# Feed-forward stage: the forms of x in the activations' tiles, made at the beginning, and pair 3 by seven products

## The chip, the cores and the metric

The kernel runs on one core of a Trainium2 chip. The metric is the device time of one launch in microseconds. The engines are named as in the profile: PE is TensorE, PEld its weight loads, DVE is VectorE, ACT is ScalarE, POOL is GpSimd, and SP is the engine that issues most loads.

## The reference

The reference is a trunk of two layers on 512 tokens with 1024 features, all in fp32. In each layer come a mixer (attention in layer 0, an mLSTM in layer 1), a cross-attention to 256 memory tokens, and a gated feed-forward network with a short convolution. Only the last part is touched:

```python
def conv_ffn(xn, w_up, conv_w, conv_b, w_down):
    h = causal_depthwise_conv(xn @ w_up, conv_w) + conv_b   # w_up: 1024 x 5632, 3 taps
    g, u = jnp.split(h, 2, axis=-1)
    return (jax.nn.gelu(g) * u) @ w_down                    # w_down: 2816 x 1024
...
        x = x + conv_ffn(rms_norm(x, ffn_norm[layer]), ffn_w_up[layer], ffn_conv_w[layer],
                         ffn_conv_b[layer], ffn_w_down[layer])
```

## The kernel before

Features lie on the partitions and the 512 tokens on the free axis, so `x` is eight tiles of 128 x 512. Every product of fp32 matrices is made of three matmuls (`mm3`): both operands are split into a rounded high part and a rest, and high x high, high x rest and rest x high are summed. The high part is a cast on ACT, the rest a subtraction on DVE.

The up projection has 5632 columns, taken as 22 pairs: pair p has the 128 gate columns of block p and the 128 linear columns of block 22 + p. A pair is computed in one of two ways.

`plain(p, fill)` makes two blocks of output, 128 features x 512 tokens each, over eight blocks of the input: 2 x 8 x 3 matmuls of 512 columns. Each weight block is loaded, cast and split (1024 columns), and each sum is evacuated on DVE with the norm's factor.

`seven(p, fill)` treats the pair as a product of two matrices of 2 x 2 blocks (two halves of the input features and two of the output, two halves of the tokens) and computes it with seven products of blocks in place of eight, in Winograd's form. A product is 4 x 3 matmuls of 256 columns. Its weights are A11 and A12 (`raw`, `f3`), S1 and S3 (`sa`, `f1`: a load, and a second load that POOL adds onto it in memory), S2 and S4 (`s2`, `s4`, formed on DVE in `sb`) and A22 (`a22`, loaded into `ra`). The results go through PSUM and the small sums `v`, `u2`, `u3`, `c11`, `c12`, `c21`, `c22` into `hs`, which one DVE instruction then scales with the norm's factor. The products `p1` to `p7` use half of the tokens of `xh`/`xl` (p1, p2, p3) or of the forms T1 to T4 of x (p4 to p7).

`forms(k, at)` makes these forms for the input blocks k and k + 4, once per layer: two scalings on ACT, sums and differences on DVE, a cast into `th[k]` and a subtraction into `tl[k]`. Before the change the scaled blocks lie in a tile of `hs` (two of them, which the pairs use in turn), and the sums in a tile of `sa` (three, which hold the loads of S1 and S3 for the seven pairs). `p6` of each seven pair waits for all forms, and so do the additions of the down projection to x.

`tail(p, ...)` follows each pair: the three taps (one on ACT, four instructions `c` at L1314 on DVE), gelu, the product, and the split into the activations' tiles `ah` and `al`, of which there are ten each. `down(c, m)` multiplies a chunk of four (the last one: six) of these by a block of the down projection and adds to x. Down projections of chunk 0 to 3 are put between the products of pairs from 5 on (`fill`), two to a pair as long as the queue has any; `due` says at which pair a chunk joins the queue. The last five wait till the pairs are done, and chunk 4 comes at the end.

The order of the work is planned twice. `Sched` is a list scheduler in Python: every step is a task on one engine with a duration, a due time, its dependences and the buffers that it takes (`act`=10, `hs`=2, `sa`=3, `h`=3 and others) in the order in which the tasks were added; it issues what can start first, by due time among equals. The framework then puts the instructions on the engines in that order of priority, where an instruction whose inputs are ready may pass an earlier one that waits, and tiles of a new stage may be filled as soon as the tiles of the old stage in the same memory are read for the last time. The tiles of the feed-forward stage are laid out in the order `th`, `tl`, `s2`, `a22`, `s4`, `ah`/`al`, `hs`, and then the others.

Before the change pairs 0 to 3 are plain and pairs 4 to 21 go by seven products. The forms are asked for behind pairs 0 and 1:

```python
        for p in range(22):
            ...
            (seven if p in SEVEN else plain)(p, fill if p >= 5 else lambda: None)
            if p < 2:
                for k in (2 * p, 2 * p + 1):
                    forms(k, clock[0] + 4.0 * (k % 2))
```

Of the kernel before, what the change touches and what calls it, by code (L numbers as in the profile page):

```python
# [9 lines left out]
F32 = mybir.dt.float32  # L10
F32R = mybir.dt.float32r
I32 = mybir.dt.int32
AF = mybir.ActivationFunctionType
ALU = mybir.AluOpType
# [8 lines left out]
NPAIR = DFF // P  # L23
CHUNKS = [(0, 4), (4, 4), (8, 4), (12, 4), (16, 6)]

SEVEN = (4, 5, 6, 7, 8, 9, 10, 11, 12, 13, 14, 15, 16, 17, 18, 19, 20, 21)
EPS = 1e-6

X_AT, X_STEP = 2.6, 0.6
# [32 lines left out]
class Plan:  # L62
# [11 lines left out]
    def add(self, fn, dur=0.0, deps=(), prio=None, take=(), free=(), chain=(), pre=(), after=0.0, order=(), load=(), st=None):  # L74
        it = Item(fn, dur, [d for d in deps if d is not None], len(self.items) if prio is None else prio, take, free, chain, pre, after, order, load, st)
        it.n = len(self.items)
        self.items.append(it)
        return it
# [151 lines left out]
class Builder:  # L230
# [924 lines left out]
    def ffn_steps(self, layer, mp):  # L1155
# [3 lines left out]
        nc, t = self.nc, self.t  # L1159
        sc = Sched(raw=3, h=3, s2=1, s4=1, a22=1, sa=3, sb=2, ra=1, hs=2, c=1, dr=2, v=1, u2=1, u3=1, act=10, acc=4, s=2, w=2)  # L1160
        add = sc.add
        tt = lambda n: 0.055 + 1.06e-3 * n
        act = lambda n: 0.1 + 0.83e-3 * n
        ACV, STT = 0.71, 0.66
        clock = [0.0]
        state = {}
        acts, acted = {}, {}
        HALF = [slice(0, 256), slice(256, 512)]
        pair = lambda a: a.rearrange("p (a b) -> p a b", a=2)
# [10 lines left out]
        def raw_tile(st, tag):  # L1180
            pool, n, bufs = RAWS[tag]
            st[tag] = self.til(pool, tag, (P, n), bufs=bufs)
            return st[tag]
# [76 lines left out]
        th, tl = ([mp.tile([P, 1024], F32R, name=f"t{i}{layer}{k}", tag=f"t{i}{k}") for k in range(4)] for i in "hl")  # L1260
        small_ = lambda tag: [self.til(mp, tag + i, dtype=F32R, bufs=1) for i in "hl"]
        act_ = lambda: tuple(self.til(mp, i, dtype=F32R, bufs=10) for i in ("ah", "al"))
# [5 lines left out]
        formed = []  # L1268
        hs2 = [mp.tile([P, 2, 514], F32, name=f"hs{layer}{i}") for i in range(2)]
# [2 lines left out]

        def forms(k, at):

            st = {}

            def scaled(j):
                if j == 0:
                    st["t"] = hs2[st["_hs"]][:, :, 2:514]
                nc.scalar.activation(st["t"][:, j, :512], self.x[k + 4 * j][:], AF.Identity, scale=self.col("ffn", layer * 8 + k + 4 * j))  # L1280

            def first():
                st["r"] = raw_tile(st, "sa")[:]
                tt_(out=pair(st["r"][:, :512]), in0=pair(st["t"][:, 0, :512]), in1=st["t"][:, :, 256:512], op=ALU.subtract)

            T1, T3, T2, T4 = (slice(256 * i, 256 * i + 256) for i in range(4))
            tt_ = nc.vector.tensor_tensor
            a = add("ACT", ACV, lambda: scaled(0), (), at, [("hs", st)])
            a = add("ACT", ACV, lambda: scaled(1), [a], at)
            a = add("DVE", tt(512), first, [a], at, [("sa", st)])  # L1290
            a = add("DVE", tt(256), lambda: tt_(out=st["r"][:, T2], in0=st["t"][:, 1, 256:512], in1=st["r"][:, T1], op=ALU.add), [a], at)
            a = add("DVE", tt(256), lambda: tt_(out=st["r"][:, T4], in0=st["t"][:, 1, 0:256], in1=st["r"][:, T2], op=ALU.subtract), [a], at, (), [("hs", st)])
            h = add("ACT", act(1024), lambda: nc.scalar.copy(th[k][:], st["r"]), [a], at)
            formed.append(add("DVE", tt(1024), lambda: self.sub(tl[k][:], st["r"], th[k][:]), [h], at, (), [("sa", st)]))


        def tail(p, st, deps, at):
# [187 lines left out]

        normed = None
        due = {4 * c + 5 + c // 3: c for c in range(4)}
        for p in range(22):
            if p in due:
                queue += [(due[p], m) for m in range(8)]  # L1490
            if p == 19:
                queue, late = queue[:-5], queue[-5:]
            (seven if p in SEVEN else plain)(p, fill if p >= 5 else lambda: None)
            if p < 2:
                for k in (2 * p, 2 * p + 1):
                    forms(k, clock[0] + 4.0 * (k % 2))
        queue += late
        while queue:
            fill()
        if layer == 0:  # L1500
            for m in range(8):
                e = down(4, m, 2)
                a = add("ACT", 1.2, lambda m=m: self.xprep(m, "mix", 1, state), [e], clock[0] + 3.0)
# [371 lines left out]
```

## Time and profile before

| | |
|---|---|
| time, median of 3 runs | 1487.87 us (1487.7 to 1488.3) |
| profiled execution: own time | 1488.21 us |
| profiled execution: span from first to last instruction | 1486.4 us |
| mean granted TensorE clock | 0.999 |
| busy PE / DVE / ACT / POOL | 1474.2 / 1207.3 / 814.7 / 61.6 us |
| first matmul of the feed-forward stage, layer 0 / layer 1 | 416.05 / 1134.68 us |

The profile is one execution. Times of the trace count from its first instruction. The page has a line for each engine with its busy time in 40 equal slices of the span, each digit a tenth; a timeline row has the start in us, the duration in us, the engine, the line of the kernel, the operation, output and inputs, and in brackets the idle time of the engine before it and what ended that. Many rows have the line of a helper: L284 to L286 are the three matmuls of `mm3`, L275 is the subtraction of every split.

### The profile page before, as it was taken

How to read it: one execution, taken by the hardware profiler on the slowest of the kernel's cores; microseconds unless marked ns; L12 is line 12 of the kernel's file. 1: busy time of each engine (PE TensorE's matmuls, PEld its weight loads, DVE VectorE, ACT ScalarE, POOL GpSimd, SP SyncE). 2: the span in 40 equal slices, each digit the busy share in tenths (PEclk: the TensorE clock that was granted, in tenths of full speed). 3: DMA queues.
4: the chain of work that ended last, by engine and by line, in shares of the span. 5: the costliest groups of instructions: out<-in, count | busy, mean ns of one | idle time of the engine just before them, and what ended most of it. 6: DMA issues, size and time to landing. Idle time of an engine off the chain costs nothing.

```text
span 1486.4 us, 22787 instructions
## 1 busy us (share of the span) xinstructions
PE 1474.2 (99%) x8570; PEld 1276.6 (86%) x8570; DVE 1207.3 (81%) x2332; ACT 814.7 (55%) x1372; POOL 61.6 (4%) x104
## 2 busy tenths in 40 slices
PE   9999999999999999999999999999999999999998
PEld 7888777888888999999888778888888899999987
DVE  7779795666679999999768857666567999999984
ACT  7777573444456555555446634444444655555554
POOL 0000130000001000000000000000000000000000
PEclk9999999999999999999999999999999999999999
DMA  5212223323237565662322222323323666656422
GB/s 196 86 63 79 86 79 121 122 78 128 72 131 201 163 150 168 157 157 77 92 96 86 71 99 77 108 85 119 123 71 121 169 171 157 171 154 160 117 67 78
DMA packets 62463, 174.94 MB, mean 118 GB/s; under 512 B 6800, under 2 KB 6800, under 8 KB 62352
## 3 DMA queue, kind: packets, MB, share of 16 engines
q1 hardware_dynamic: 56160, 153.48, 31.4%
q0 software_dynamic: 5184, 18.88, 7.5%
q8 instruction: 67, 1.10, 0.3%
q10 hardware_dynamic: 1008, 1.12, 0.2%
q14 instruction: 44, 0.36, 0.1%
HBM read 171.35 MB, written 2.10 MB: 117 GB/s over the span
## 4 chain that ended last, share of the span: by engine, by line
PE 81%; DVE 13%; ACT 2%; issue 2%; DMA 1%; ACTq 0%; DVEq 0%; SPq 0%
PE acc L284 16%; PE acc L285 16%; PE acc L286 16%; PE w L286 4%; PE w L284 4%; PE w L285 4%; DVE wl L275 3%; PE acc L345 3%; PE acc L347 2%; PE acc L346 2%; PE s L284 2%; PE s L285 2%; PE s L286 2%; DVE c L1314 2%; PE w L1660 1%
## 5 line engine op out<-in xcount | busy, mean ns | idle before, releaser
L284 PE MATMUL acc<-xh,wh 128*128 128x512 f32 (+1 forms) x800 | 284.2, 355 | 0.0
L286 PE MATMUL acc<-xh,wl 128*128 128x512 f32 (+1 forms) x800 | 279.6, 349 | 0.0
L285 PE MATMUL acc<-xl,wh 128*128 128x512 f32 (+1 forms) x800 | 279.4, 349 | 0.0
L275 DVE TENSOR_TENSOR wl<-raw,wh 128x1024 fp32r<-128x1024 f32 (+4 forms) x199 | 235.5, 1184 | 41.0 <-ACT wh L278 39.2
L278 ACT CAST wh<-raw 128x1024 fp32r<-128x1024 f32 (+1 forms) x135 | 139.4, 1035 | 162.7 <-PE acc L285 98.0
L286 PEld LDWEIGHTS acc<-xh,wl 128*128 128x128 f32 x800 | 150.2, 188 | 20.1
L285 PEld LDWEIGHTS acc<-xl,wh 128*128 128x128 f32 x800 | 150.4, 188 | 19.9
L284 PEld LDWEIGHTS acc<-xh,wh 128*128 128x128 f32 x800 | 150.3, 188 | 19.8
L1314 DVE SCALAR_TENSOR_TENSOR c<-hs,vec,c 128x512 f32<-128x512 f32 x176 | 129.5, 744 | 0.3
L286 PE MATMUL w<-ah,wl 128*128 128x512 f32 x304 | 119.0, 391 | 0.0
L284 PE MATMUL w<-ah,wh 128*128 128x512 f32 x304 | 118.7, 390 | 0.0
L285 PE MATMUL w<-al,wh 128*128 128x512 f32 x304 | 118.6, 390 | 0.0
L1307 ACT ACTIVATE c<-hs,vec 128x512 f32<-128x512 f32 x88 | 70.2, 813 | 46.9 <-DVE hs L1457 41.8
L1202 ACT CAST wh<-dr 128x512 fp32r<-128x512 f32 x64 | 39.5, 618 | 51.8 <-PE acc L285 16.7
L286 PEld LDWEIGHTS w<-ah,wl 128*128 128x128 f32 x304 | 57.1, 188 | 12.0
L284 PEld LDWEIGHTS w<-ah,wh 128*128 128x128 f32 x304 | 57.1, 188 | 10.5 <-ACT ah L1328 0.6
L285 PEld LDWEIGHTS w<-al,wh 128*128 128x128 f32 x304 | 57.1, 188 | 10.0
L284 PE MATMUL acc<-mem,wh 128*128 128x256 f32 (+1 forms) x192 | 61.5, 320 | 0.0
L286 PE MATMUL acc<-mem,wl 128*128 128x256 f32 (+1 forms) x192 | 61.0, 318 | 0.0
L285 PE MATMUL acc<-mem,wh 128*128 128x256 f32 (+1 forms) x192 | 60.8, 317 | 0.0
L526 DVE TENSOR_TENSOR x<-acc,x 128x512 f32<-128x512 f32 x32 | 22.1, 691 | 46.9 <-PE acc L286 46.9
L526 DVE TENSOR_TENSOR x<-w,x 128x512 f32<-128x512 f32 x72 | 49.2, 684 | 12.2 <-PE w L286 11.6
(390 smaller groups left out, 3950.7 us busy)
## 6 DMA issues: line engine op xcount, KB each, us to landing
raw<-in_up_dram SPq DMA_DIRECT2D x52, 512.0 KB, 3.4
sa<-in_up_dram SPq DMA_DIRECT2D x36, 512.0 KB, 4.3
sa<-in_up_dram POOLq DMA_DIRECT2D x36, 512.0 KB, 5.6
dr<-in_down_dram SPq DMA_DIRECT2D x64, 256.0 KB, 3.3
ra<-in_up_dram SPq DMA_DIRECT2D x36, 256.0 KB, 3.1
raw<-in_xk_dram SPq DMA_DIRECT2D x16, 512.0 KB, 3.3
raw<-in_wo_dram SPq DMA_DIRECT2D x16, 512.0 KB, 3.3
raw<-in_xq_dram SPq DMA_DIRECT2D x16, 512.0 KB, 3.3
```

The costliest lines, as they stand in the source:

```text
L275: self.nc.vector.tensor_tensor(out=lo, in0=v, in1=hi.bitcast(F32), op=ALU.subtract)
L278: self.nc.scalar.copy(hi, v)
L284: mm(out, wh, xh, start=first, stop=False, skip_group_check=parts)
L285: mm(out, wh, xl, start=False, stop=False, skip_group_check=parts)
L286: mm(out, wl, xh, start=False, stop=last, skip_group_check=parts)
L345: mm(ps, xh[k][:, ts], wh[:, ws], start=(k == 0), stop=False)
L346: mm(ps, xh[k][:, ts], wl[:, ws], start=False, stop=False)
L347: mm(ps, xl[k][:, ts], wh[:, ws], start=False, stop=(k == 7))
L526: self.nc.vector.tensor_tensor(out=self.x[m][:], in0=ps[:], in1=self.x[m][:], op=ALU.add)
L1202: nc.scalar.copy(st["wh"][:, :cols], st[tag][:, :cols])
L1307: nc.scalar.activation(st["c_"][:, j, :], hs()[:, j, 2:514], AF.Identity, scale=self.col("cw", (layer * 3 + 2) * 44 + blk), bias=self.col( ...
L1314: nc.vector.scalar_tensor_tensor(out=c, in0=hs()[:, j, n : n + 512], scalar=w, in1=c, op0=ALU.mult, op1=ALU.add)
```

## The change

Pair 3 is added to the pairs that go by seven products: 19 of 22. The forms are asked for ahead of all pairs, with due times 2, 4, 6 and 8. They take two of the ten tile pairs `ah`/`al` each in place of a tile of `hs` and one of `sa`: the first for the two scaled blocks, given back after the sums, the second for the sums. The four sums are four instructions of 256 columns (before: one of 512 and two of 256). The cast into `th` and the subtraction into `tl` are done in two halves of 512 (before: one of 1024 each).

```diff
-SEVEN = (4, 5, 6, 7, 8, 9, 10, 11, 12, 13, 14, 15, 16, 17, 18, 19, 20, 21)
+SEVEN = tuple(range(3, 22))
...
         def forms(k, at):
 
-            st = {}
+            st, su = {}, {}
+            two = lambda: [a[:].bitcast(F32) for a in act_()]
+            L, R = HALF
+            tt_ = nc.vector.tensor_tensor
 
             def scaled(j):
                 if j == 0:
-                    st["t"] = hs2[st["_hs"]][:, :, 2:514]
-                nc.scalar.activation(st["t"][:, j, :512], self.x[k + 4 * j][:], AF.Identity, scale=self.col("ffn", layer * 8 + k + 4 * j))
+                    st["t"] = two()
+                nc.scalar.activation(st["t"][j], self.x[k + 4 * j][:], AF.Identity, scale=self.col("ffn", layer * 8 + k + 4 * j))
 
             def first():
-                st["r"] = raw_tile(st, "sa")[:]
-                tt_(out=pair(st["r"][:, :512]), in0=pair(st["t"][:, 0, :512]), in1=st["t"][:, :, 256:512], op=ALU.subtract)
-
-            T1, T3, T2, T4 = (slice(256 * i, 256 * i + 256) for i in range(4))
-            tt_ = nc.vector.tensor_tensor
-            a = add("ACT", ACV, lambda: scaled(0), (), at, [("hs", st)])
+                su["r"] = two()
+                t, r = st["t"], su["r"][0]
+                tt_(out=r[:, L], in0=t[0][:, L], in1=t[0][:, R], op=ALU.subtract)
+                tt_(out=r[:, R], in0=t[0][:, R], in1=t[1][:, R], op=ALU.subtract)
+
+            def second():
+                t, (r, q) = st["t"], su["r"]
+                tt_(out=q[:, L], in0=t[1][:, R], in1=r[:, L], op=ALU.add)
+                tt_(out=q[:, R], in0=t[1][:, L], in1=q[:, L], op=ALU.subtract)
+
+            a = add("ACT", ACV, lambda: scaled(0), (), at, [("act", st)])
             a = add("ACT", ACV, lambda: scaled(1), [a], at)
-            a = add("DVE", tt(512), first, [a], at, [("sa", st)])
-            a = add("DVE", tt(256), lambda: tt_(out=st["r"][:, T2], in0=st["t"][:, 1, 256:512], in1=st["r"][:, T1], op=ALU.add), [a], at)
-            a = add("DVE", tt(256), lambda: tt_(out=st["r"][:, T4], in0=st["t"][:, 1, 0:256], in1=st["r"][:, T2], op=ALU.subtract), [a], at, (), [("hs", st)])
-            h = add("ACT", act(1024), lambda: nc.scalar.copy(th[k][:], st["r"]), [a], at)
-            formed.append(add("DVE", tt(1024), lambda: self.sub(tl[k][:], st["r"], th[k][:]), [h], at, (), [("sa", st)]))
+            a = add("DVE", 0.68, first, [a], at, [("act", su)])
+            b = add("DVE", 0.68, second, [a], at, (), [("act", st)])
+            for i, c in enumerate((a, b)):
+                w = slice(512 * i, 512 * i + 512)
+                c = add("ACT", act(512), lambda i=i, w=w: nc.scalar.copy(th[k][:, w], su["r"][i]), [c], at)
+                last = add("DVE", tt(512), lambda i=i, w=w: self.sub(tl[k][:, w], su["r"][i], th[k][:, w]), [c], at, (), [("act", su)] if i else ())
+            formed.append(last)
...
         due = {4 * c + 5 + c // 3: c for c in range(4)}
+        for k in range(4):
+            forms(k, 2.0+2.0*k)
         for p in range(22):
...
-            if p < 2:
-                for k in (2 * p, 2 * p + 1):
-                    forms(k, clock[0] + 4.0 * (k % 2))
```

## Prediction

> **What bounds the kernel now.** I read the page first, then the waits of TensorE (PE), then busy time by stretches of the first feed-forward stage, then single instructions.
>
> ```profile
> PE 1474.2 (99%) x8570; PEld 1276.6 (86%) x8570; DVE 1207.3 (81%) x2332; ACT 814.7 (55%) x1372; POOL 61.6 (4%) x104
> DVE  7779795666679999999768857666567999999984
> PE acc L284 <- DVE u L1433: 0.7, 4, 0.2
> ```
>
> PE is busy for 99% of the span, and the only thing in the two feed-forward stages that it is ever said to wait for is `u` on VectorE (DVE), four times. But the tenths of DVE stand at 9 through both feed-forward stages (slices 12 to 18 and 32 to 37), so two engines are full there at once. The stretches of layer 0 show where exactly; the columns are stretch, length, then busy time of PE, PEld, DVE, ACT and POOL, clock, DMA share and GB/s.
>
> ```profile
> 416.00:427.00 11.00, 11.00 (x53) 8.90 (x52) 9.79 (x26) 5.93 (x8) 0.00 (x0) 1.00 0.43 139
> 427.00:438.00 11.00, 11.00 (x50) 9.03 (x49) 9.37 (x15) 8.53 (x12) 0.00 (x0) 1.00 0.24 88
> 438.00:449.00 11.00, 11.00 (x50) 9.11 (x49) 10.05 (x16) 7.58 (x10) 0.69 (x1) 1.00 0.42 143
> 449.00:461.00 12.00, 12.00 (x54) 9.95 (x53) 12.00 (x18) 7.05 (x9) 1.17 (x2) 1.00 0.86 220
> 480.00:500.00 20.00, 20.00 (x147) 18.61 (x147) 19.99 (x35) 11.47 (x18) 0.86 (x1) 1.00 0.54 139
> 560.00:580.00 20.00, 20.00 (x143) 18.57 (x142) 20.00 (x35) 10.90 (x18) 1.71 (x2) 1.00 0.61 175
> 580.00:600.00 20.00, 20.00 (x151) 18.89 (x151) 19.61 (x36) 11.31 (x19) 0.85 (x1) 1.00 0.62 158
> 680.00:705.00 25.00, 24.92 (x206) 24.12 (x205) 24.99 (x43) 14.81 (x24) 0.00 (x0) 1.00 0.19 64
> 1145.60:1156.50 10.90, 10.90 (x49) 8.93 (x48) 9.29 (x15) 8.39 (x12) 0.00 (x0) 1.00 0.25 89
> ```
>
> PE is never idle here. DVE has 1.21 + 1.63 + 0.95 = 3.8 us to spare between 416 and 449, while the plain pairs run, then none up to 580, a little (0.39) in the stretch after, and none in 680 to 705. The layer 1 row shows the same picture (1.61 us spare). So a saving on PE counts in full only if DVE, which this change loads more, does not fall behind.
>
> **What the change removes on PE.** A plain pair is 48 wide matmuls, a pair by seven products 84 narrow ones (7 products, 4 blocks, 3 matmuls each).
>
> ```profile
> 442.21 0.39 PE L284 MATMUL acc<-xh,wh 128*128 128x512 f32 x1
> 447.65 0.39 PE L284 MATMUL acc<-xh,wh 128*128 128x512 f32 x1
> 1191.28 0.28 PE L284 MATMUL s<-xh,s4h 128*128 128x256 f32 x1
> 1192.64 0.28 PE L284 MATMUL s<-th,wh 128*128 128x256 f32 x1
> ```
>
> The first two rows are 24 wide matmuls apart: 5.44 us, 227 ns each, so a plain pair takes 10.88 us. The last two are one product of 12 narrow matmuls apart: 1.36 us, 113 ns each, so seven take 9.52 us. Pair 3 saves 1.36 us in each layer, 2.72 in all. This is the whole gain that PE can give, 0.18% of the time. The Trainium skill (TensorE: Matmul & The Clock Gate, section "Back-to-back issue gap") says that in a stream of weight loads and matmuls the spacing is about 131 ns at 512 columns and 81 ns at 128, so that narrow ones cost more for each column; by a straight line between (98 ns at 256, my estimate) pair 3 would become 84 x 98 - 48 x 131 = 1.9 us longer. This trace disagrees, with 227 and 113 ns.
>
> **What it adds on PE.** The pair that runs without down projections between its products (`fill` starts at pair 5) waits for its own sums:
>
> ```profile
> 469.56 1.21 DVE L275 TENSOR_TENSOR wl<-sa,wh 128x1024 fp32r<-128x1024 f32 x1
> 470.70 0.41 DVE L1433 TENSOR_TENSOR u<-acc,v 128x256 f32<-128x256 f32 x1
> 471.03 0.68 DVE L1324 TENSOR_TENSOR c<-c 128x512 f32<-128x512 f32 x1
> 470.71 0.28 PE L286 MATMUL acc<-th,s2l 128*128 128x256 f32 x1
> 471.16 0.39 PE L284 MATMUL acc<-th,a22h 128*128 128x256 f32 x1 [0.18 <-DVE u L1433]
> ```
>
> Between the last two rows 0.45 us pass where 0.11 would do: 0.34 us lost in pair 4, because `u3` stood behind a weight split on DVE. Now pairs 3 and 4 both run without down projections. I count the stall a second time: 0.34 in each layer, 0.68 in all, with bounds of nothing (the order may fall better) and twice that. A gain below nothing is excluded by no row, as the old stall may go too: that is a rival below.
>
> **What it adds on DVE.** The spacings of instructions that stand back to back, as each record overlaps the next a little:
>
> ```profile
> 474.17 0.68 DVE L275 TENSOR_TENSOR a22l<-ra,a22h 128x512 fp32r<-128x512 f32 x1
> 474.77 0.41 DVE L1433 TENSOR_TENSOR hs<-s,u 128x256 f32<-128x256 f32 x1
> 475.10 0.67 DVE L275 TENSOR_TENSOR s4l<-sb,s4h 128x512 fp32r<-128x512 f32 x1
> 475.70 1.21 DVE L1457 TENSOR_TENSOR hs<-hs,rb 128x1024 f32<-128x1024 f32 x1
> 476.84 0.41 DVE L1433 TENSOR_TENSOR u<-acc,v 128x256 f32<-128x256 f32 x1
> ```
>
> So 0.33 us for 256 columns, 0.60 for 512, 1.14 for 1024 (the split at 469.56 too). A plain pair has two splits of 1024 and two evacuations of 512: 3.48 us. A seven pair has two sums and three splits of 512, two splits of 1024, five sums of 256 and one scaling of 1024: 5 x 0.60 + 2 x 1.14 + 5 x 0.33 + 1.14 = 8.07. The taps are the same. That is +4.6 a layer. A form was 0.60 + 2 x 0.33 + 1.14 = 2.40 and becomes 4 x 0.33 + 2 x 0.60 = 2.52: +0.5 for four. DVE gets 5.1 us more in each layer, against 1.36 saved on PE.
>
> ```profile
> 462.90 0.36 ACT L1428 ACTIVATE v<-acc 128x256 f32<-128x256 f32 x1
> 463.16 0.61 ACT L1384 CAST s4h<-sb 128x512 fp32r<-128x512 f32 x1
> ```
>
> ScalarE gets three casts of 512, `v` and a copy of 256 more, 3 x 0.61 + 2 x 0.36 = 2.6 us; at 7.05 busy of 12.00 before pair 4 that is covered. SP gets the loads of pair 3 in other shapes, and POOL one more accumulating DMA.
>
> **What covers the DVE work: the move of the forms.** Where they run now, and why:
>
> ```profile
> L1271 POOL MEMSET hs<- x4: 102/103/103, 382.0 to 1132.0; 128x4 f32 x4
> L1280 ACT ACTIVATE hs<-x,vec x16: 706/716/722, 417.0 to 1166.3; 128x512 f32<-128x512 f32 x16
> 413.38 0.10 POOL L1271 MEMSET hs<- 128x4 f32 x1 [31.24 <-PE acc L285]
> 410.81 0.69 DVE L526 TENSOR_TENSOR x<-acc,x 128x512 f32<-128x512 f32 x1 [2.09 <-PE acc L286]
> 416.25 0.69 DVE L526 TENSOR_TENSOR x<-acc,x 128x512 f32<-128x512 f32 x1 [2.09 <-PE acc L286]
> 442.10 1.22 DVE L275 TENSOR_TENSOR tl<-sa,th 128x1024 fp32r<-128x1024 f32 x1
> 443.38 5.45 SPq L1188 DMA_DIRECT2D sa<-in_up_dram  x2
> ```
>
> Each tile waits for memory of the stage before. The first `hs` tile is free at 382.0, the second at 413.38, so the first form starts at 417.0 and the others queue behind `hs` slots that the pairs hold. The activations' tiles are laid out ahead of `hs`, over memory of the same attention tiles, so I take them to be free by about 382. Then a form can start when its two `x` are final. `x` 6 is written at 410.81, `x` 7 at 416.25, the ones before every 5.44 us; and DVE stands idle for 2.09 us in each such step. Four sums of 256 (1.32 us) fit into that. Forms 0 to 2 would put 4.0 us of DVE work before 416, where it costs nothing. The splits into `th` and `tl` cannot go there, since these tiles lie over what the last output projection still reads. What is left, 5.1 - 4.0 = 1.1 us a layer plus the 1.36 that PE gains, has the 3.8 us idle of 416 to 449 for cover. I price the DVE load at nothing. If neither cover were there it would be 5.1 a layer. The `sa` slots are also freed: today pair 4's load at 443.38 waits for a form's last read of `sa` (442.10 + 1.22), so pair 3's loads can go early.
>
> **The sum**: -2.72 + 0.68 = -2.04. The profiled execution's own time is 1488.21 us, so 1486.17; it stands 0.34 above the median of the runs, 1487.87, so 1485.8 as a median.
>
> **The rivals.** *DVE becomes the bound (slower).* Tiles come free too late or the order puts the forms' sums where DVE is full, and pairs 3 and 4, each 8.07 us and taps on top, run behind each other with no down projection to stretch them. For it: no idle DVE from 449 to 580. Against: the idle stretches above. It decides when more than 3.8 of the 5.1 us find no gap; then PE waits for `u`, `s2` and `hs`. With no move ahead of 416 and half of the idle time used, 5.1 - 1.9 = 3.2 a layer arrive late, 6.4 in all, which replaces the gain, as DVE then sets the end: 1494.3. Up to 1498.1 with no cover.
>
> *The entry of the stage is delayed (slower).*
>
> ```profile
> 417.60 0.71 ACT L506 ACTIVATE xh<-x,vec 128x512 fp32r<-128x512 f32 x1
> 418.34 0.75 DVE L507 SCALAR_TENSOR_TENSOR xl<-x,vec,xh 128x512 fp32r<-128x512 f32 x1
> 416.05 0.39 PE L284 MATMUL acc<-xh,wh 128*128 128x512 f32 x1
> ```
>
> Pair 0 needs `xl` 7 after seven blocks of 0.68 us, at 420.8; it is there at 419.1. If the six casts into `th` of forms 0 to 2 go ahead of `xh` 7 (form 3 needs `x` 7 itself), 6 x 0.61 = 3.7 us against 1.7 of slack, PE waits 2.0 a layer: 1485.8 + 4.0 = 1489.8. Against: `xh` 7 comes earlier in the program.
>
> *The gain is eaten.* Pair 3 waits for its own splits or the last `tl`, and DVE is that much later in 680 to 705, where it has nothing to spare: 0 to 1.4 a layer lost, time about 1487.2.
>
> *More gain than PE's share.* Freed `sa` slots and earlier forms also take away the 0.34 of pair 4 and the other waits for `u` (0.7 in all on the page): -2.72 - 1.4 - some ordering luck, 1483.7.
>
> *Narrow products bound by the weight load.* Were each spaced by the load's busy time (1276.6 us over 8570 loads, 149 ns on average), pair 3 would take 12.5 us, +1.6 a layer: 1491.1. The skill's rule above leans that way; the spacing of 113 ns in the 18 pairs that run so already leaves it 1%.
>
> **How the numbers follow.** Forecast 60%; eaten gain 15%; DVE bound 13%; entry delayed 5%; more gain 6%; weight load 1%. A difference under 0.2% (3 us) is about what a measurement of this kernel cannot tell from none, and PE's share is below it, so forecast and eaten gain are both "same": 0.75, faster 0.07, slower 0.18. The range leaves out the DVE bound and the larger gain (19%); its low end is PE's whole share with no second stall, 1485.1, less 0.5 for the spread of runs, its high end the weight load's price: 1484.6 to 1491.1.
>
> **What would show it.** Right: the matmuls with `th` number 19/18 of now; first sums of forms from about 400; DVE idle before 416 shrunk; PE waits for `u` still about 0.2 each. Wrong: PE gaps of over 1 us between 445 and 480 that end on DVE (`s2l`, `tl`, `u`), or a last `tl` after 451.

## The result: slower by 3.4 us, just above the range

The kernel after takes 1491.53 us (median of 10 runs, 1490.81 to 1493.35), the kernel before 1488.12 in the same runs: a ratio of 1.0024, 95% interval 1.0016 to 1.0032. The forecast was 1485.8, the range ended at 1491.1. TensorE (PE) does what was forecast, and VectorE (DVE) takes it back and more. The page of after, busy time and DVE's tenths:

```profile
PE 1474.5 (99%) x8642; PEld 1279.5 (86%) x8642; DVE 1215.5 (82%) x2366; ACT 821.4 (55%) x1390; POOL 64.5 (4%) x106
DVE  7779795666689999999778857666567999999984
```

PE runs 72 matmuls more, 84 narrow ones for 48 wide ones in each layer, in the same busy time (1474.2 before). A matmul's record (0.39 us) is longer than the spacing to the next start (0.227), so a start that is late by less than that still shows as busy. DVE has 8.2 us more (1207.3 before). The page hardly shows the damage. The stretches of layer 0 do (stretch, length, busy time of PE, PEld, DVE, ACT, POOL, clock, DMA share, GB/s), first two of the kernel before, then those of the kernel after:

```profile
405.00:416.00 11.00, 11.00 (x50) 9.13 (x49) 6.36 (x8) 4.40 (x6) 0.10 (x1) 1.00 0.31 109
461.00:480.00 19.00, 18.82 (x151) 18.06 (x150) 18.90 (x34) 11.89 (x20) 2.55 (x3) 1.00 0.85 215
```

```profile
405.00:416.00 11.00, 11.00 (x50) 9.11 (x49) 6.36 (x8) 4.42 (x7) 0.10 (x1) 1.00 0.34 110
416.00:427.00 11.00, 11.00 (x53) 9.03 (x52) 10.15 (x32) 10.77 (x18) 2.72 (x3) 1.00 0.97 282
427.00:438.00 11.00, 11.00 (x50) 9.06 (x49) 11.00 (x21) 8.29 (x12) 0.00 (x0) 1.00 0.74 182
438.00:449.00 11.00, 11.00 (x50) 9.12 (x49) 11.00 (x18) 6.02 (x8) 0.00 (x0) 1.00 0.28 95
449.00:461.00 12.00, 11.75 (x95) 11.18 (x93) 11.86 (x18) 7.81 (x12) 0.86 (x1) 1.00 0.46 115
461.00:480.00 19.00, 18.28 (x142) 17.40 (x143) 18.86 (x34) 9.12 (x17) 1.71 (x2) 1.00 0.69 183
```

Three things are to be seen. DVE's 3.8 us of idle time between 416 and 449 have shrunk to 0.85. The stretch ahead of 416 has not filled: 6.36 us of 11, with 8 instructions, as before. And behind 449 PE is now idle for 0.25 and 0.72 us in the last two stretches; before it was for nothing and for 0.18. What it waits for stands in PE's waits (us in total, times, longest), of which the first line is new:

```profile
PE s L286 <- DVE wl L275: 2.0, 4, 0.6
PE acc L284 <- DVE u L1443: 0.4, 2, 0.2
```

The four waits are one in pair 4 and one in pair 5 of each layer, before the first matmul of `p5` that reads `wl`, the low part of the split of `sa`. The first of them on PE, ScalarE and DVE:

```profile
460.47 0.28 PE L285 MATMUL acc<-xl,wh 128*128 128x256 f32 x1
461.15 0.38 PE L286 MATMUL s<-th,wl 128*128 128x256 f32 x1 [0.40 <-DVE wl L275]
455.78 1.05 ACT L1394 CAST wh<-sa 128x1024 fp32r<-128x1024 f32 x1 [0.67 <-PE acc L285]
457.41 0.74 DVE L1324 SCALAR_TENSOR_TENSOR c<-hs,vec,c 128x512 f32<-128x512 f32 x1
458.07 0.69 DVE L275 TENSOR_TENSOR s2l<-sb,s2h 128x512 fp32r<-128x512 f32 x1
458.67 0.68 DVE L1334 TENSOR_TENSOR c<-c 128x512 f32<-128x512 f32 x1
459.27 0.69 DVE L1406 TENSOR_TENSOR sb<-sb,raw 128x512 f32<-128x512 f32 x1
459.88 1.22 DVE L275 TENSOR_TENSOR wl<-sa,wh 128x1024 fp32r<-128x1024 f32 x1
```

The cast that `wl` needs is done at 456.83; `wl` starts 3.05 us later, behind a sum `u`, a tap, a split, the product with the gate and a sum into `sb`. DVE has no idle time between these rows: it is a backlog.

To sum this up I take the feed-forward stages from the start of the first matmul to that of the last:

| | layer 0 | layer 1 |
|---|---|---|
| before | 416.05 to 755.97: 339.92 us | 1134.68 to 1475.90: 341.23 us |
| after | 416.01 to 756.76: 340.75 us | 1135.72 to 1478.44: 342.71 us |

The matmuls of the change take 1.36 us less in each layer at 227 ns (512 columns) and 113 ns (256 columns) from start to start. So what lies between starts beyond these spacings, PE's lost time, grew by 2.2 us in layer 0 and 2.8 in layer 1. That is 5.0 more, against 2.72 saved: 2.3. The first matmuls of the last group and the final stores, before and then after:

```profile
1478.14 1.95 PE L1723 MATMUL acc<-ident,x 128*128 128x128 f32 x16
1478.24 3.97 SPq L1732 DMA_DIRECT2D out_dram<-tl  x4
```

```profile
1480.67 1.94 PE L1732 MATMUL acc<-ident,x 128*128 128x128 f32 x16
1480.78 4.88 SPq L1741 DMA_DIRECT2D out_dram<-tl  x4
```

The group starts 2.53 us later. The span grew by 3.9 us in these two executions (1486.4 to 1490.3), so 1.3 us lie behind the last matmuls. The final stores' issue takes 0.9 us longer of it in this execution; in the other kernels' it is between 3.6 and 4.7 us without any order that fits, and the cause of these 1.3 us is not shown.

### The profile page after: what moved, and what is told of

The parts are those of the page before. It is cut to its first block, busy times and chain, and to the rows that moved or that the text cites. A ratio compares the mean times of both kernels' runs of the same rounds, so it can differ in the third digit from the quotient of the medians.

```text
span 1490.3 us, 23013 instructions
## 1 busy us (share of the span) xinstructions
PE 1474.5 (99%) x8642; PEld 1279.5 (86%) x8642; DVE 1215.5 (82%) x2366; ACT 821.4 (55%) x1390; POOL 64.5 (4%) x106
## 4 chain that ended last, share of the span: by engine, by line
PE 82%; DVE 12%; ACT 3%; issue 2%; DMA 1%; POOL 0%; SPq 0%; ACTq 0%; POOLq 0%; DVEq 0%
PE acc L284 16%; PE acc L285 16%; PE acc L286 16%; PE w L286 5%; PE w L284 5%; PE w L285 5%; DVE wl L275 3%; PE s L286 2%; PE s L284 2%; PE acc L345 2%; PE s L285 2%; PE acc L347 2%; PE acc L346 2%; DVE c L1324 1%; PE w L1669 1%
## 5 line engine op out<-in xcount | busy, mean ns | idle before, releaser
L284 PE MATMUL acc<-xh,wh 128*128 128x512 f32 (+1 forms) x784 | 277.3, 354 | 0.1
L286 PE MATMUL acc<-xh,wl 128*128 128x512 f32 (+1 forms) x784 | 271.8, 347 | 0.0
L285 PE MATMUL acc<-xl,wh 128*128 128x512 f32 (+1 forms) x784 | 271.3, 346 | 0.0
L275 DVE TENSOR_TENSOR wl<-raw,wh 128x1024 fp32r<-128x1024 f32 (+3 forms) x197 | 233.3, 1184 | 41.1 <-ACT wh L278 39.4
L284 PEld LDWEIGHTS acc<-xh,wh 128*128 128x128 f32 x784 | 147.3, 188 | 20.2 <-ACT wh L1394 0.6
L286 PEld LDWEIGHTS acc<-xh,wl 128*128 128x128 f32 x784 | 147.2, 188 | 19.1
L285 PEld LDWEIGHTS acc<-xl,wh 128*128 128x128 f32 x784 | 147.4, 188 | 18.7
L284 PEld LDWEIGHTS w<-ah,wh 128*128 128x128 f32 x304 | 57.1, 188 | 10.2 <-ACT ah L1338 0.6
```

The costliest lines, as they stand in the source:

```text
L275: self.nc.vector.tensor_tensor(out=lo, in0=v, in1=hi.bitcast(F32), op=ALU.subtract)
L284: mm(out, wh, xh, start=first, stop=False, skip_group_check=parts)
L285: mm(out, wh, xl, start=False, stop=False, skip_group_check=parts)
L286: mm(out, wl, xh, start=False, stop=last, skip_group_check=parts)
```

## The experiments

The theory, T1: pair 3's further 4.6 us of DVE work in each layer meet too little idle time, the splits of pairs 4 and 5 come late, and PE waits. T2: the move of the forms is what costs. T3: not DVE's load, but the form of a pair by seven (casts, single buffers, slots). Others are named where they came up. Each kernel's median is set beside the kernel before in the same runs (1488.1 to 1488.25) and beside the kernel after (1491.5).

**The two parts alone.** The move of the forms without pair 3, which is the kernel after with

```
-SEVEN = tuple(range(3, 22))
+SEVEN = tuple(range(4, 22))
```

> The changed kernel with pair 3 as a plain pair again: only the forms are moved to the beginning of the stage and into the activations' tiles. T1 (the time went to VectorE, which cannot take pair 3's 4.6 us a layer beside pairs 4 and 5): 1487.5 to 1488.7, no wait of TensorE for a weight split wl of over 0.3 us. T2 (the move of the forms, which puts four forms between 417 and 434, is what costs): 1489.5 to 1491.5. If neither VectorE nor the move matters (T3): 1488.

Measured: 1487.05 us, ratio to before 0.9994 (0.9985 to 1.0003). T2 is out: the move costs nothing and brings about 1 us. PE waits for `u` only once, and the stretches show why: DVE has time to spare again.

```profile
438.00:449.00 11.00, 11.00 (x51) 9.09 (x50) 10.23 (x15) 4.67 (x6) 0.00 (x0) 1.00 0.48 143
461.00:480.00 19.00, 19.00 (x154) 18.46 (x153) 18.62 (x32) 12.17 (x20) 1.71 (x2) 1.00 0.68 166
```

Pair 3 by seven without the move, which is the kernel before with

```
-SEVEN = (4, 5, 6, ...
+SEVEN = (3, 4, 5, 6, ...
```

> The kernel before with pair 3 by seven products and the forms where and as they were. T1: the same 4.6 us a layer meet less free VectorE time, so 1489 to 1492, with waits of TensorE for VectorE of 2 us or more between 445 and 480. T2: 1485.2 to 1486.2, the saving of 2.72 us in full.

Measured: 1508.45 us, ratio 1.0135 (1.0121 to 1.0149), 16.5 us above T1's range. The direction is T1's, the size is something else. DVE's and PE's instructions around the long wait:

```profile
456.38 1.22 DVE L275 TENSOR_TENSOR wl<-sa,wh 128x1024 fp32r<-128x1024 f32 x1
462.04 0.69 DVE L1390 TENSOR_TENSOR sb<-sa,raw 128x512 f32<-128x512 f32 x1 [4.45 <-DMA sa<-in_up_dram]
462.65 0.68 DVE L275 TENSOR_TENSOR s2l<-sb,s2h 128x512 fp32r<-128x512 f32 x1
459.18 0.41 PE L284 MATMUL s<-th,wh 128*128 128x256 f32 x1
463.39 0.58 PE L286 MATMUL acc<-th,s2l 128*128 128x256 f32 x1 [3.80 <-DVE s2l L275]
463.77 0.42 PE L284 MATMUL acc<-th,s2h 128*128 128x256 f32 x1
463.99 0.41 PE L285 MATMUL acc<-tl,s2h 128*128 128x256 f32 x1
```

Here DVE is idle for 4.45 us, at the head of its queue a sum of pair 4 that waits for a load into `sa`, and behind it the `s2l` of pair 3 that PE needs. So without the move the slots of `sa`, which the forms hold, are the bound. Then the two rows after the wait: 0.22 us apart instead of 0.113; on that in the last section. To see whether it is the slots (T8), the same kernel with four of them, and for the memory nine tile pairs `ah`/`al`:

```
-... sa=3, ... act=10, ...
+... sa=4, ... act=9, ...
```

> The kernel of pair 3 alone (forms as before, 1508.45) with four sa slots instead of three, and for the memory nine pairs of activations' tiles instead of ten. T8 (what cost 20 us there is that the forms sit in sa slots, so that the loads of pairs 3 and 4 come late and VectorE waits for one of them with pair 3's s2l behind it): the waits for s2l of 3.8 us go, and the time falls to 1490 to 1496, the rest being T1's VectorE load. If it were VectorE's load alone (T1 without T8): 1505 or more, unchanged.

Measured: 1499.43 us (1498.4 to 1500.9), ratio 1.0076 (1.0062 to 1.0090). The waits for `s2l` are gone and with them 9.0 of the 20.3 us, so T8 holds for this half; the rest stands between the two expectations. PE's waits name it:

```profile
PE s L284 <- ACT wh L1384: 2.8, 2, 1.4
PE s L286 <- DVE wl L275: 2.0, 2, 1.0
```

ScalarE's casts of pair 3's weights are late. Ahead of them in its queue stand, from 451.3 on, the last form's cast into `th`, `v`, two instructions of a pair's tail, and a copy into `hs` that itself waits for PE; which of these costs the time was not tested. The parts do not add: the forms' move alone -1.05, pair 3 alone +20.3, both +3.4. The move is what makes pair 3 by seven bearable at all, by 16.9 us; it is not enough.

**The load by itself.** On the kernel of the forms alone, pair 3 stays plain, and each of its two weight splits is made three times:

```
-... own, clock[0], "acc", (), 2)
+... own, clock[0], "acc", (), 2, times=3 if p == 3 else 1)
```

> The kernel of the forms alone (pair 3 plain, 1487.05 before), with each of the two weight splits of pair 3 made three times over: four further splits of 1024 columns, 4 x 1.14 = 4.6 us more VectorE work in each layer, which is what the seven products add there, and nothing changed on TensorE. T1 (VectorE is the bound at pairs 3 to 5): it sets the end whatever TensorE saves, so the time is that of the changed kernel, 1490 to 1492.5. T3 (it is the form of a pair by seven, its casts, single buffers and slots): 1487 to 1488.

Measured: 1492.00 us (1491.6 to 1492.4), ratio 1.0026 (1.0015 to 1.0036). This is the experiment that decides. No pair has changed its form, so T3's cause is absent; the same DVE work at the same place gives the same time as the change, within half a microsecond. The two feed-forward stages are 3.1 and 2.7 us longer than in the kernel without the load (341.96 and 343.01 us, against 338.88 and 340.29). PE waits partly for other tiles, all of them VectorE's:

```profile
PE acc L284 <- DVE u L1443: 1.5, 3, 0.7
PE acc L286 <- DVE wl L275: 0.8, 2, 0.4
PE s L286 <- DVE wl L275: 0.6, 2, 0.4
```

The repeated splits also hold their raw tile longer, but VectorE waits for no load there: it is busy for the whole of 449 to 461. So 4.6 us a layer cost 4.95 in both layers together. What the 2.72 that PE saves buy back in the change is less sure: 0.5 us in the medians, which is inside the intervals, and 1.7 between the last groups of matmuls of the two traces.

**Relief, at the place and elsewhere.** The kernel after without the forms' sums:

```
-            a = add("DVE", 0.68, first, [a], at, [("act", su)])
-            b = add("DVE", 0.68, second, [a], at, (), [("act", st)])
...
+                c = add("ACT", act(512), lambda i=i, w=w: nc.scalar.copy(th[k][:, w], st["t"][i]), [a], at)
```

> The changed kernel without the 16 sums that make a layer's forms (the scaled blocks are split as they are, so this part of the computation is left out): VectorE gets 16 x 0.33 = 5.3 us less in each layer between 417 and 434, TensorE's work is the same. T1: the waits for wl in pairs 4 and 5 fall under 0.5 us in all, and the time is 1485 to 1486.5. T3 (the casts on ScalarE, the single buffers of s2, s4 and a22 or the down projections' tiles are what pairs 3 and 4 wait for): 1490 to 1492.

Measured: 1487.33 us, ratio 0.9993 (0.9984 to 1.0002). The waits for `wl` are gone; 5.3 us less a layer give back 4.2 us. T3 is out a second time. The edit also frees one of the two tile pairs that a form takes, which this run does not tell apart; the load alone does. But the time is 0.8 above T1's range: it is the kernel of the forms alone again (1487.05), so in the medians pair 3 still brings nothing (0.6 us between the last groups of matmuls). The same 5.3 us, later:

```
-                for n in (1, 0):
+                for n in (1, 0)[: 1 if p in range(9, 13) else 2]:
```

> The changed kernel with the last tap of the convolution left out in pairs 9 to 12 (8 x 0.66 = 5.3 us less VectorE work in each layer, as much as the forms' sums were, but later; this part of the computation is left out). T1 (the loss is made at pairs 4 and 5): no more than the small losses behind pair 8 come back, 1490 to 1491.5. Rival T4 (VectorE is short over the whole stage, whose busy share is 99%, so that any relief counts): 1487 to 1488.5.

Measured: 1490.42 us, ratio 1.0015 (1.0007 to 1.0024): 1.1 us for what brings 4.2 at the beginning. T4 is out. VectorE's busy share of the whole stage says little; it is 96% in layer 0 and 94% in layer 1 of the kernel after, not the 99% of the expectation. Between 100 and 260 us of the stage PE loses only 0.6 us more in layer 0 than in the kernel of the forms alone, so little can be won there.

Is the gain of pair 3 there when DVE is out of the way? Two kernels, the kernel after and the one of the forms alone, each without the last tap in pairs 0 to 7 (`range(8)` in the line above):

> The changed kernel with the last tap left out in pairs 0 to 7: 16 x 0.66 = 10.6 us less VectorE work in each layer where the stage is tight (this part of the computation is left out). T1: with VectorE out of the way pair 3's 2.72 us appear in full against the same relief of the kernel with the forms alone: 1483.5 to 1485. Rival T5 (a pair by seven at this place costs TensorE its gain by waits that no spare VectorE time removes): no more than 0.7 us under that kernel, 1486 to 1487.

> The kernel of the forms alone (pair 3 plain) with the last tap left out in pairs 0 to 7, the same relief and the same part of the computation left out as in the run before it. T1: TensorE hardly waits there already, so little changes against 1487.05: 1486 to 1487, and the other run lies 2 to 3 us under it. T5: the two are within 0.7 us.

Measured: 1486.05 (1485.0 to 1486.6) and 1486.80 us (1486.3 to 1487.3), ratios 0.9985 (0.9976 to 0.9994) and 0.9990 (0.9981 to 0.9999). The difference is 0.75 in the medians and 1.5 between the last groups of matmuls of the two traces, where T1 expected 2 to 3: both theories hold half. What is left is not the backlog alone. Pair 4 with the taps left out, DVE then PE:

```profile
468.66 0.42 DVE L1443 TENSOR_TENSOR u<-acc,v 128x256 f32<-128x256 f32 x1
469.00 0.68 DVE L1334 TENSOR_TENSOR c<-c 128x512 f32<-128x512 f32 x1
469.60 0.42 DVE L1443 TENSOR_TENSOR hs<-u,s 128x256 f32<-128x256 f32 x1
469.52 0.28 PE L285 MATMUL acc<-tl,a22h 128*128 128x256 f32 x1
470.07 0.38 PE L284 MATMUL s<-xh,s4h 128*128 128x256 f32 x1 [0.27 <-DVE hs L1443]
```

The product with `s4` takes the bank that `hs<-u,s` empties, that needs `u`, and `u` needs the product before. Without down projections only products of the next pair can run meanwhile, and one foreign instruction of 0.60 us between the two DVE steps is a stall of 0.43. In these two pairs PE loses 0.8 us in each layer, where the kernel with a plain pair 3 loses nothing.

**Place and order.** Did the forms miss the idle time ahead of 416 only for their due time? The kernel after with

```
-            forms(k, 2.0+2.0*k)
+            forms(k, k - 40.0)
```

> The changed kernel with the forms due 40 us before the stage begins instead of 2 to 8 us into it, so that the stage's own list puts them ahead of every weight cast. If they are late because of their due time (T7), the first scaled block comes at about 400, right after its second x, three forms' sums (4.0 us of VectorE) go into the idle stretches before 416, and the time is 1487 to 1489. T1 with its reading of the failed step (whatever lies in the stage's own tiles is placed behind the stage before, so no due time helps): the first scaled block again at 416 to 417.6, and 1490.5 to 1492.5.

Measured: 1491.15 us (1490.3 to 1492.0). The first scaled block, by the line's record in this run, then ScalarE around it in the kernel after:

```profile
L1283 ACT ACTIVATE ah<-x,vec x8: 708/716/722, 416.7 to 1145.6; 128x512 f32<-128x512 f32 x8
```

```profile
415.98 1.05 ACT L1202 CAST wh<-raw 128x1024 fp32r<-128x1024 f32 x1 [3.24 <-PE acc L285]
416.94 0.72 ACT L1283 ACTIVATE ah<-x,vec 128x512 f32<-128x512 f32 x1
417.57 0.71 ACT L506 ACTIVATE xh<-x,vec 128x512 fp32r<-128x512 f32 x1
```

T7 is out: asked for first, it comes at 416.7. In the instruction list it keeps its place, between the cast that waits for the stage before and the last `xh`; casts of the new stage's weights into tiles that are older than the stage do run from 405 on. It fits that whatever writes a tile of the new stage is lined up behind the readers of the stage before, whenever its memory is really free. The counter-test, forms in a tile from outside the stage, was not tried, so this stays an inference.

Is it capacity or only the order (T6)? The taps of pairs 1 to 4 due 10 us later in the kernel after:

```
-... lambda j=j, n=n: tap(j, n), [a], at + 4.0)
+... lambda j=j, n=n: tap(j, n), [a], at + (14.0 if p in (1, 2, 3, 4) else 4.0))
```

> The changed kernel with the convolution's taps of pairs 1 to 4 due 10 us later, so that weight splits and sums of pairs 3 to 5 go ahead of them where both are ready: the work is the same, the order on VectorE is not. T1 (VectorE's capacity): what is put off comes back as later down projections, and the time stays at 1490.5 to 1492.5. T6 (it is only the order, taps ahead of the split wl that TensorE waits for): 1487.5 to 1489.5.

Measured: 1490.16 us (1489.0 to 1491.4), ratio 1.0013 (1.0004 to 1.0022): between the two, nearer to T1. The waits for `wl` stand as before, 2.0 us; what falls are small losses between 60 and 80 us of the stage. The same edit with pair 3 plain, as a version that might beat both kernels:

> The two edits that helped, together: the forms moved as in the change, pair 3 plain as before, and the taps of pairs 1 to 4 due 10 us later. T1: without pair 3's further work VectorE has room at pairs 3 to 5, so the order of the taps matters little and the time is that of the forms alone, 1486.5 to 1487.3, about 1 us under the kernel before and 4 to 5 us under the changed one. T6 (order is what costs): 1485.5 to 1486.4, as the 1.4 us that the later taps gave the changed kernel come on top.

Measured: 1488.02 us, ratio 0.9998 (0.9989 to 1.0007), 1.0 above the forms alone: T6 is out, and T1's figure missed by 0.7. In the trace pair 7 waits 0.3 us a layer more for the sum `hs<-u,s`; another 0.9 us arise ahead of the first feed-forward stage, where the two kernels are the same, so differences of about 1 us are not safely the edit's. The forms alone remain the best version: 4.5 us under the kernel after, and 1.05 under the kernel before, an interval that just includes no difference.

**The other engine.** GpSimd (POOL) is 4% busy. The kernel after with its forms' sums and `tl` there:

```
-            tt_ = nc.vector.tensor_tensor
+            tt_ = nc.gpsimd.tensor_tensor
...
-            a = add("DVE", 0.68, first, [a], at, [("act", su)])
+            a = add("POOL", 1.2, first, [a], at, [("act", su)])
...
```

> The changed kernel with the forms' sums and the subtractions that make tl on GpSimd: VectorE gets 16 x 0.33 + 8 x 0.60 = 10 us less in each layer at the place in question. T1: 1484.8 to 1486.5, waits for wl gone. T3: 1490 or more. Under either, if GpSimd is so slow that the last tl comes after pair 3's first use of it (about 443), or if it keeps the accumulating loads that it issues waiting, TensorE waits for tl or for sa instead, and the time is over 1490: the trace would show that by name.

Measured: 1522.76 us, ratio 1.0234 (1.0220 to 1.0248). It says nothing on T1, as it failed in a way that no theory had: DVE stopped.

```profile
421.48 0.16 DVE L420 TENSOR_SCALAR z<-s 128x4 f32<-128x4 f32 x1 [1.15 <-PE s L1245]
421.67 9.10 DVE L421 TENSOR_SCALAR y<-z 128x4 int32<-128x4 int32 x1
430.69 0.16 DVE L422 TENSOR_SCALAR zh<-z 128x4 f32<-128x4 f32 x1
429.48 1.25 POOL L1289 TENSOR_TENSOR ah<-ah,al 128x256 f32<-128x256 f32 x1
433.60 0.79 PE L467 MATMUL s<-sqt,ones 128*128 128x512 f32 x1 [9.09 <-DVE sqt L461]
```

An instruction of 0.16 us takes 9.10 and ends with the last of a run of GpSimd instructions (429.48 + 1.25 = 430.73). The norm comes 9 us late, and PE waits for it. With layer 1 that is 18 of the 34.6 us. Two waits of about 3 us for `v` behind it, and matmuls at half speed after these waits, belong to the rest, which was not taken apart.

## Why the prediction was wrong

- **PE's share was right.** The matmuls with `th` went from 144 to 152 of each kind, 19/18, and the spacings of 227 and 113 ns held; the rival of the weight load did not occur.
- **The second stall** was put at 0.34 us a layer for a wait for `u`. In the kernel after the waits are others, for `wl`. With DVE relieved the two pairs without down projections lose 0.8 us in a layer, against 0.34 + 0.34 in the prediction: the term was right in kind and a little small.
- **DVE's 5.1 us a layer** were about right. Busy time grew by 8.2 us in two layers where 10.2 were due, but records that overlap hide a part: the run with the load alone, 9.2 us by the same spacings, shows 7.6 more than the kernel without it (1216.1 and 1208.5). And these 4.6 us a layer by themselves gave the change's time.
- **The step that failed is "I price the DVE load at nothing".** It rested on two covers. The first, 4.0 us of the forms' sums ahead of 416, did not exist: memory free at 382 does not put an instruction there, and the row of 405 to 416 is the same before and after. The prediction had read when the tiles' memory came free and not where the instructions stood in ScalarE's queue, although its own rows of before showed the same thing, the first form at 417.0 with its `hs` tile free at 382.0. The second cover, 3.8 us idle from 416 to 449, was real, and 2.9 of it were used up. So 5.1 - 2.9 = 2.2 us a layer arrived late, and PE's lost time grew by 2.2 in layer 0 and by 2.8 in layer 1. That these agree so well in layer 0 is in part luck, as the lost time also holds the stalls between dependent products.
- Even with that cover the forecast would hardly have come: without the sums (5.3 us a layer) the time is 1487.33, what the rival of the eaten gain said (1487.2). The gain of 2.72 needs a DVE with time to spare and something for PE to do between dependent products, and pairs 3 and 4 have neither.
- **The rival "DVE becomes the bound" was the right one**, with a chance of 13% and a price too high. It was said to decide when more than 3.8 of the 5.1 us find no gap; 2.2 were enough. Its 6.4 us late in all replaced the gain, for 1494.3; with the 4.4 that were late by the idle rows the same sum gives 1492.3 as a median, close to the 1491.5 measured.
- The signs named ahead came in part. Of those for a right forecast, the matmuls with `th` came as said, but the sums from about 400 and the shrunk idle time before 416 did not. Of those for a wrong one, gaps on PE between 445 and 480 that end on DVE came, though of 0.4 to 0.6 us each and on `wl`; the last `tl`, at 433.6, was in time.

## What to carry to other kernels

Before trading one engine's work for another's, look for idle time of the engine that gets it in the very stretch, and count only what lies behind the place where its instructions stand in the queue: free memory and an early due time moved nothing here. Two engines that are both full are one bound, and a saving on the first counts for what the second leaves of it; one run with the second engine's further work alone shows that price. When a part of a change seems harmless by itself, test the other part alone too: here the move of the forms was worth 1 us alone, hardly more than the noise, and 17 with pair 3.

## What the runs showed of the hardware

**Waits on TensorE can halve its clock.** In the kernel with pair 3 alone matmuls of 256 columns start 0.21 us apart instead of 0.113 for 4.7 us after the wait of 3.80. The granted clock of these stretches:

```profile
449.00:461.00 12.00, 7.00 (x43) 5.74 (x41) 8.40 (x12) 6.18 (x10) 1.71 (x2) 0.89 0.86 211
461.00:480.00 19.00, 16.61 (x122) 16.43 (x122) 15.81 (x24) 9.42 (x15) 1.71 (x2) 0.80 0.78 181
```

That wait is not alone: the same spacing stands in the rows from 458.5 to 459.2, ahead of it, behind four shorter waits. With four `sa` slots these four come without the long one. None is over 1.6 us (0.95, 1.57, 0.61 and 1.14 us longer between starts than the usual, within 7 us), and they brought the same for 3 us. A long wait with no such row of others before it stands in the kernel with the sums on GpSimd, first its rows, then the stretch behind it:

```profile
466.67 0.28 PE L286 MATMUL s<-th,wl 128*128 128x256 f32 x1
470.28 0.58 PE L284 MATMUL acc<-xh,wh 128*128 128x256 f32 x1 [3.34 <-ACT v L1438]
470.66 0.41 PE L285 MATMUL acc<-xl,wh 128*128 128x256 f32 x1
470.30:475.70 5.40, 5.40 (x25) 5.40 (x26) 5.03 (x8) 2.38 (x5) 0.00 (x0) 0.50 0.77 134
```

The waits of the kernel after, two of 0.4 and 0.6 us ten apart, left the clock at 1.00. The Trainium skill (TensorE: Matmul & The Clock Gate, "Part 1: The HAM clock gate") says that the clock falls to half after an idle window of about 3.4 us and comes back after as long a busy one. The traces agree on the half and roughly on the time, 3 to 5.5 us until it is back. That several short waits do it too fits a measure of the activity in a window rather than of one gap.

**GpSimd can hold VectorE up.** The Trainium skill (SBUF — State Buffer, "SBUF: two separate sides") says that the two share a pair of ports, which one of them holds for a whole instruction. The 9.10 us for 0.16 agree with the lock and go beyond the instruction: nine further GpSimd instructions started while VectorE's one waited. Not every VectorE instruction is held: in the same run `hs<-acc,rb` at 440.90 took its usual 0.69 us beside a running GpSimd instruction, and the tap right behind it 5.27 instead of 0.74. Nor was GpSimd fast: its records of a sum of 256 columns are 0.9 to 1.1 us on average and start 0.68 apart, where VectorE's record is 0.42.
